# The gate product of an encoder layer as one Strassen level over pairs of token tiles, with the residual tiles kept in memory

## The chip, the core and the metric

One core of a Trainium2 chip runs one layer as one program. The metric is the device time of an execution in microseconds (us); lower is better. The engines work side by side, each through its own list of instructions in order: TensorE (PE in the rows) multiplies matrices into PSUM, VectorE (DVE), ScalarE (ACT) and GpSimd (POOL) do elementwise work, and SyncE (SP) issues the transfers between memory and SBUF. Semaphores order work between engines. All lists are laid down when the program is built, in the order in which the Python code calls the operations.

## The reference: what is computed

```python
xn = rms_norm(x, norm_g[i])
proj = jnp.einsum('bsd,de->bse', xn, w_in[i])
...
oa = diff_attention(q1, q2, k1, k2, va_h, lam, t5_bias)
...
yb = neighbourhood_attention(qb, kb, vb, na_rpb[i]) * jax.nn.silu(zb)
y = jnp.einsum('bse,ed->bsd', jnp.concatenate([ya, yb], axis=-1), w_out[i])
x = x + y
gate = jax.nn.sigmoid(jnp.einsum('bsd,de->bse', x, w_ple_gate[i]))
x = x + gate * jnp.einsum('bsp,pd->bsd', p[i], w_ple_proj[i])
```

There is one batch of 1024 tokens, the model has 1024 columns, and all data are float32. The change concerns the last two lines: the gate product is 1024x1024 by 1024x1024. The residual after the output projection (`x + y`) is called x1 below.

## The kernel before

Every float32 matmul is made of three: an operand is split into a rounded high part and a low part (high by an ACT copy into the type float32r, low by a DVE subtraction), and high x high, high x low and low x high are added up in PSUM. The 1024 tokens are eight tiles of 128. The input projection, neighbourhood attention and differential attention come first. The rest of the program, from about 680 us on, is this:

- `outb` has left the second half of the output projection plus x in a memory tensor `xpd[t]` for each token tile t, with a store `xpd<-oev` for each half tile.
- `outa(t)` loads `xpd[t]` as a tile named x, runs 24 matmuls (`oap`, 128x512 each) for the first half of the output projection, and adds both on DVE (L1231). The result is x1 of that tile, and it stays in SBUF.
- `load_wg` and `split_wg` bring the gate's weights in eight tiles `wgr` of 128x1024 and split them into `wgh` and `wgl`.
- `x1_trans(t)` transposes x1 in eight matmuls with the identity (`x1p`) and splits it into `x1h` and `x1l`.
- `gate(t)` runs, for each half of the columns (c), 24 matmuls into a PSUM tile `gps`, then a tanh on ACT (L1261), then two DVE operations (L1262 with the tile `ppl`, which is half of the embedding's projection and is loaded from memory, and L1263 with x1), and a store to the output.

The order is written out by hand: a loop over t calls `x1_trans(t - 5)`, `gate(t - 6)` and `outa(t)`. SBUF tiles come from pools with a fixed number of buffers for each size; a load into a buffer waits until the last reader of its former content is through. All loads and stores of this stretch are issued by SP, in the order of the code, and SP holds at an instruction whose semaphores have not come.

Of the kernel before, what the change touches and what calls it, by code (L numbers as in the profile page):

```python
# [40 lines left out]
def layer_kernel(ctx, tc, x, p, ngr, w_in, w_out, gains, lamv, t5p, rpbp, w_gate, w_ple,  # L41
# [1155 lines left out]
    wgh = []  # L1197
    wgl = []
    wgr = {}

    def load_wg(kc):
        wgr[kc] = T4([P, D], n="wgr")
        ld(wgr[kc], w_gate[kc * P:(kc + 1) * P, :])

    def split_wg(kc):
        if kc % 2 == 0:
            wgh.append(T8([P, 2, D], F32R, n="wgh"))
            wgl.append(T8([P, 2, D], F32R, n="wgl"))
        r = wgr.pop(kc)
        h, l = wgh[kc // 2], wgl[kc // 2]  # L1210
        act(h[:, kc % 2], r, AF.Copy)
        zl.append(lambda: V.tensor_tensor(l[:, kc % 2], r, h.bitcast(F32)[:, kc % 2], op=OP.subtract))
# [4 lines left out]
    def outa(t):  # L1217
# [14 lines left out]
        x1[t] = xt  # L1232

    def x1_trans(t):
        xt = x1[t]
        h = T4([P, 8, P], F32R, n="x1h")
        l = T4([P, 8, P], F32R, n="x1l")
        for g in range(2):
            tp = PS([P, 4, P], "x1p")
            for k in range(4):  # L1240
                kc = 4 * g + k
                nc.tensor.transpose(tp[:, k], xt[:, kc * P:(kc + 1) * P], idn)
            act(h[:, 4 * g:4 * g + 4], tp, AF.Copy)
            V.tensor_tensor(l[:, 4 * g:4 * g + 4], tp, h.bitcast(F32)[:, 4 * g:4 * g + 4], op=OP.subtract)
        x1T[t] = (h, l)

    def gate(t):
        h, l = x1T.pop(t)
        xt = x1.pop(t)
        for c in range(2):  # L1250
            cs = slice(c * 512, c * 512 + 512)
            pp = T2([P, 512], n="ppl")
            ld(pp, ppd[t][:, cs])
            ps = PS([P, 512], "gps")
            for k in range(8):
                wh, wl = wgh[k // 2][:, k % 2, cs], wgl[k // 2][:, k % 2, cs]
                mm(ps, h[:, k], wh, start=(k == 0), stop=False)  # L1257
                mm(ps, h[:, k], wl, start=False, stop=False)  # L1258
                mm(ps, l[:, k], wh, start=False, stop=(k == 7))  # L1259
            th = T2([P, 512], n="gth")  # L1260
# [76 lines left out]
    for i in range(1, NI + 6):  # L1337
# [39 lines left out]
        if i >= 34:  # L1377
            for kc in (2 * (i - 34), 2 * (i - 34) + 1):
                load_wg(kc)
                if i > 34:  # L1380
                    split_wg(kc - 2)
# [75 lines left out]
```

## Time and profile before

| what | us |
|---|---|
| median of 3 runs | 836.67 |
| the runs, lowest to highest | 835.38 to 838.21 |
| time of the profiled execution | 838.91 |
| its span, first to last instruction | 837.1 |
| TensorE busy in the span | 783.7 (94%) |
| DVE, ACT, POOL busy | 511.8, 437.6, 266.2 |

The profiled execution took 1.81 us more than its span, and 2.24 us more than the median of the runs. Times in the rows below are microseconds from the start of the span. A matmul's shown duration includes its way through the pipeline; how fast matmuls follow each other is read from their starts.

### The profile page before, as it was taken

Reading aid. Unit: us, or ns where it says so; the run is one execution under the profiler, and the core shown is the slowest. Engines: PE = TensorE matmul, PEld = TensorE weight load, DVE = VectorE, ACT = ScalarE, POOL = GpSimd, SP = SyncE. Lnnn points to the kernel's source line nnn. Section 1 sums busy time; section 2 is a strip of 40 time slices with the busy share of each in tenths; the row PEclk is TensorE's granted clock in tenths of the full one; section 3 lists DMA queues with packets and bytes.
Section 4 is the critical chain, followed back from the end, with each engine's and each line's share of the span. In section 5 each row is a group of like instructions: output and inputs, shape, how many; then the busy total and the mean of one; then the engine's idle time right before and its main releaser. Section 6 shows DMA issues by size and latency. Waiting matters only on the chain.

```text
span 837.1 us, 12190 instructions
## 1 busy us (share of the span) xinstructions
PE 783.7 (94%) x4242; PEld 649.8 (78%) x4242; DVE 511.8 (61%) x986; ACT 437.6 (52%) x814; POOL 266.2 (32%) x267
## 2 busy tenths in 40 slices
PE   7899799999989994998979998999999999999997
PEld 6678588888878883776767776888888877888886
DVE  4557795685997662653635658777777752732332
ACT  5665355255435532554545569889888861411120
POOL 1003443261565400110101124677776761200000
PEclk9999899999999997999999999999999999999999
DMA  8655461945788999576666768757686437223222
GB/s 330 272 175 172 170 186 59 325 128 132 173 280 241 217 298 235 140 178 180 200 168 183 175 206 225 216 154 209 163 236 174 144 124 268 85 76 101 83 94 88
DMA packets 118525, 151.94 MB, mean 181 GB/s; under 512 B 23832, under 2 KB 76728, under 8 KB 118336
## 3 DMA queue, kind: packets, MB, share of 16 engines
q1 hardware_dynamic: 116672, 145.39, 59.0%
q0 software_dynamic: 1792, 5.77, 2.2%
q8 instruction: 34, 0.56, 0.3%
q14 instruction: 27, 0.22, 0.1%
HBM read 104.96 MB, written 46.17 MB: 181 GB/s over the span
## 4 chain that ended last, share of the span: by engine, by line
PE 71%; DVE 8%; DMA 7%; ACT 5%; issue 4%; SPq 2%; POOL 2%; ACTq 0%; DVEq 0%; POOLq 0%
PE ips L232 7%; PE ips L234 7%; PE ips L233 7%; PE dsp L1064 6%; PE gps L1259 3%; PE gps L1257 3%; PE gps L1258 3%; PE dtp L1106 3%; DMA uad<-zth 3%; PE ntp L683 3%; PE pps L312 2%; PE zps L580 2%; PE zps L582 2%; PE zps L581 2%; DMA Vw<-vb 2%
## 5 line engine op out<-in xcount | busy, mean ns | idle before, releaser
L232 PE MATMUL ips<-w,xh 128*128 128x512 f32 x336 | 135.0, 402 | 5.6 <-DVE C L258 4.1
L234 PE MATMUL ips<-w,xl 128*128 128x512 f32 x336 | 132.5, 394 | 0.0
L233 PE MATMUL ips<-w,xh 128*128 128x512 f32 x336 | 132.3, 394 | 0.0
L1089 POOL TENSOR_TENSOR s<-s,s 128x1024 f32<-128x1024 f32 x32 | 77.0, 2408 | 56.9 <-ACT s L1088 52.3
L431 POOL TENSOR_TENSOR qrs<-qms,nhalf 128x16 f32<-128x16 f32 x16 | 51.7, 3233 | 91.5 <-DVE qms L429 91.5
L1074 DVE CUSTOM_DVE_ANT_0 s<-dsp,T 128x1024 f32<-128x1024 f32 x64 | 77.7, 1215 | 2.5 <-PE dsp L1064 2.5
L232 PEld LDWEIGHTS ips<-w,xh 128*128 128x128 f32 x336 | 64.2, 191 | 19.3 <-issue 4.8
L1076 ACT ACTIVATE s<-s,dm 128x1024 f32<-128x1024 f32 x64 | 73.4, 1146 | 4.6 <-DVE dm L1074 4.5
L234 PEld LDWEIGHTS ips<-w,xl 128*128 128x128 f32 x336 | 63.9, 190 | 13.9
L233 PEld LDWEIGHTS ips<-w,xh 128*128 128x128 f32 x336 | 64.2, 191 | 13.1 <-DVE w L216 0.3
L1064 PE MATMUL dsp<-K,Q 128*128 128x512 f32 x256 | 69.7, 394 | 4.9 <-DVE dm L1074 4.3
L1113 DVE TENSOR_TENSOR aTl<-dtp,aTh 128x512 fp32r<-128x512 f32 x64 | 44.2, 691 | 46.9 <-ACT aTh L1107 46.9
L714 POOL TENSOR_TENSOR yb<-nay,yb 128x128 fp32r<-128x128 f32 x32 | 16.2, 508 | 174.5 <-ACT yb L713 174.5
L216 DVE TENSOR_TENSOR w<-wraw,w 128x512 fp32r<-128x512 f32 x84 | 62.2, 778 | 5.9 <-ACT w L215 5.4
L1064 PEld LDWEIGHTS dsp<-K,Q 128*128 128x128 f32 x256 | 45.9, 189 | 14.6 <-issue 3.0
L685 ACT ACTIVATE PT<-ntp 96x768 f32<-96x768 f32 (+1 forms) x32 | 25.9, 810 | 59.2 <-PE ntp L683 59.2
L580 PE MATMUL zps<-xh,zw 128*128 128x512 f32 x128 | 54.3, 424 | 0.0
L582 PE MATMUL zps<-xh,zw 128*128 128x512 f32 x128 | 51.1, 399 | 0.0
L581 PE MATMUL zps<-xl,zw 128*128 128x512 f32 x128 | 51.0, 398 | 0.0
L215 ACT ACTIVATE w<-wraw 128x512 fp32r<-128x512 f32 x84 | 48.4, 625 | 4.7 <-DVE wraw L191 4.5
L1257 PE MATMUL gps<-wgh,x1h 128*128 128x512 f32 x128 | 50.5, 395 | 0.0
L1107 ACT ACTIVATE aTh<-dtp 128x512 fp32r<-128x512 f32 x64 | 38.0, 593 | 23.1 <-PE dtp L1106 23.1
(174 smaller groups left out, 1823.2 us busy)
## 6 DMA issues: line engine op xcount, KB each, us to landing
wraw<-in_w_in_dram SPq DMA_DIRECT2D x72, 256.0 KB
x<-in_x_dram SPq DMA_DIRECT2D x8, 512.0 KB
ppd<-pp SPq DMA_DIRECT2D x8, 512.0 KB
K<-kbh SPq DMA_DIRECT2D x8, 512.0 KB
Q<-qbh SPq DMA_DIRECT2D x16, 256.0 KB
Q<-qah SPq DMA_DIRECT2D x16, 256.0 KB
Q<-qal SPq DMA_DIRECT2D x16, 256.0 KB
wor<-in_w_out_dram SPq DMA_DIRECT2D x8, 512.0 KB
```

The lines of the kernel that those rows point to most:

```text
L216: V.tensor_tensor(w[:, 1], r, w.bitcast(F32)[:, 0], op=OP.subtract)
L232: mm(ps, lh[:, k, a:a + P], w[:, 0], start=(new and k == 0), stop=False, skip_group_check=cont)
L233: mm(ps, lh[:, k, a:a + P], w[:, 1], start=False, stop=False, skip_group_check=cont)
L234: mm(ps, ll[:, k, a:a + P], w[:, 0], start=False, stop=(k == 3), skip_group_check=cont)
L580: mm(ps, w[:, 0, kc], xh(kc, a, b), start=(kc == 0), stop=False)
L581: mm(ps, w[:, 0, kc], xl(kc, a, b), start=False, stop=False)
L582: mm(ps, w[:, 1, kc], xh(kc, a, b), start=False, stop=(kc == 7))
L1064: mm(ps[:, cs], q[g][:, m, u * P:(u + 1) * P], k[:, cs], start=(g == 0), stop=(g == 1))
L1074: V.tensor_tensor_reduce(out=s, in0=ps, in1=back(Td[h][:, :], 1919 - (896 - P * qt), [[-1, S]]), scale=-1.0, scalar=BIG, op0=OP.add, op1=O ...
L1076: act(s, s, AF.Exp, bias=mx, scale=-1.0, accum_out=z[:, m:m + 1])
L1089: G.tensor_tensor(s1, s1, s2, op=OP.add)
L1257: mm(ps, h[:, k], wh, start=(k == 0), stop=False)
```

## The change

x1 is seen as a 2x2 matrix of blocks: tile p of the first four token tiles and tile q = p + 4 of the last four give the rows, the two halves of the 1024 inputs give the columns. The gate's weights are a 2x2 matrix of quarters (B11 to B22, 512x512). The product of the two is made with one level of Strassen's scheme in Winograd's form: seven block products (P1 to P7) for eight, each 12 matmuls of 128x512, so 7 x 12 x 4 pairs = 336 matmuls take the place of 384. In return:

- Four sums of weight quarters (T1 to T4) and four sums of x1 blocks (S1 to S4) are formed, and each of the seven operands on either side is split into high and low: `g_first` (B11, B21, T1, T2), `g_second` (T3, B22, and T4 as a sum), `g_left1` to `g_left3` for the x1 side. Sums run on POOL and DVE, splits on ACT and DVE. The weights come as 16 loads of 128x512 for the first set and the same 16 again for the second set.
- Two PSUM halves A and B of one tile `gab` and one tile C (`gps`) hold the products; P6 and P7 go on top of A, P3 on top of B, P4 on top of A. Between them ACT copies A or B out (`gwv`, `gxy`), and DVE adds copies to PSUM.
- `outa(t)` stores x1 back to `xpd[t]` as soon as it is added. Tiles 0 and 4 are also used from SBUF; the other six are loaded again by `x1_load` before their transposes. The last addition of each half tile reads x1 from memory once more (`x1r`, loaded by `g_pre` beside `ppl`).

In the built program every product on `gab` waits for the last engine that read that tile, whichever half was read: P5 (which starts B) waits for the ACT copy of A behind P6, P7 (on A) for the copy of B behind P5, P3 (on B) for the copy of A behind P7, and P4 (on A) for the DVE addition behind P3.

```diff
--- before.py
+++ after.py
@@ -1194,22 +1194,48 @@
         G.tensor_tensor(yl[:, h % 2, cs], y, yh.bitcast(F32)[:, h % 2, cs], op=OP.subtract)
 
 
...
+
+
+    GLEFT = dict(P1="A11", P2="A12", P6="S2", P5="S1", P7="S3", P3="S4", P4="A22")
+    GRIGHT = dict(P1="B11", P2="B21", P6="T2", P5="T1", P7="T3", P3="B22", P4="T4")
+    gw = {}
+    gr = {}
+    gl = {}
+
+    def g_load(k, names):
+        for n in names:
+            i, j = int(n[1]) - 1, int(n[2]) - 1
+            gr[n, k] = T2([P, 512], n="wgr")
+            ld(gr[n, k], w_gate[(4 * i + k) * P:(4 * i + k + 1) * P, j * 512:(j + 1) * 512])
+
+    def g_tiles(*names):
+        for n in names:
+            gw[n] = (T8([P, 4, 512], F32R, n="wgh"), T8([P, 4, 512], F32R, n="wgl"))
+
+    def g_split(n, k, r):
+        h, l = gw[n]
+        act(h[:, k], r, AF.Copy)
+        V.tensor_tensor(l[:, k], r, h.bitcast(F32)[:, k], op=OP.subtract)
+
+    def g_first(k):
+        a, b, c, d = [gr.pop((n, k)) for n in ("B11", "B12", "B21", "B22")]
+        G.tensor_tensor(b, b, a, op=OP.subtract)
+        g_split("B11", k, a)
+        g_split("B21", k, c)
+        G.tensor_tensor(d, d, b, op=OP.subtract)
+        g_split("T1", k, b)
+        g_split("T2", k, d)
+
+    def g_second(k):
+        a, b, c, d = [gr.pop((n, k)) for n in ("B11", "B12", "B21", "B22")]
+        V.tensor_tensor(b, d, b, op=OP.subtract)
+        g_split("T3", k, b)
+        G.tensor_tensor(a, a, b, op=OP.add)
+        G.tensor_tensor(c, c, a, op=OP.subtract)
+        g_split("B22", k, d)
+        gr["T4", k] = c
+
+    QUARTERS = ("B11", "B12", "B21", "B22")
 
     x1 = {}
     x1T = {}
@@ -1229,39 +1255,126 @@
                 mm(ps, yh[:, k % 2, a:b], wl, start=False, stop=False)
                 mm(ps, yl[:, k % 2, a:b], wh, start=False, stop=(k == 3))
         V.tensor_tensor(xt, pss, xt, op=OP.add)
...
+        st(xpd[t], xt)
+        if t % 4 == 0:
+            x1[t] = xt
+
+    def x1_load(t):
+        x1[t] = TA([P, D], n="x1")
+        ld(x1[t], xpd[t])
+
+    lt = {}
+
+    def l_split(p, n, src):
+        w = T4([P, 2, 4, P], F32R, n="x1s")
+        gl[p, n] = w
+        act(w[:, 0], src, AF.Copy)
+        V.tensor_tensor(w[:, 1], src, w.bitcast(F32)[:, 0], op=OP.subtract)
+
+    def g_left1(p):
+        pa = [PS([P, 4, P], "x1p") for _ in range(2)]
+        pb = PS2([P, 2, 4, P], "x1q")
+        pts = pa + [pb[:, 0], pb[:, 1]]
+        for i in range(4):
+            xt = x1[p + 4 * (i // 2)]
             for k in range(4):
...
+                kc = 4 * (i % 2) + k
+                nc.tensor.transpose(pts[i][:, k], xt[:, kc * P:(kc + 1) * P], idn)
+        x1.pop(p)
+        x1.pop(p + 4)
+        f = TA([P, 2, 4, P], n="x1f")
+        e = TA([P, 2, 4, P], n="x1e")
+        lt[p] = (f, e)
+        act(f[:, 0], pts[0], AF.Copy)
+        act(f[:, 1], pts[1], AF.Copy)
+        act(e[:, 0], pts[2], AF.Copy)
+        V.tensor_tensor(e[:, 1], pts[3], e[:, 0], op=OP.add)
+        l_split(p, "A22", pts[3])
+        l_split(p, "A11", f[:, 0])
+        l_split(p, "A12", f[:, 1])
+        V.tensor_tensor(e[:, 0], f[:, 0], e[:, 0], op=OP.subtract)
+        l_split(p, "S1", e[:, 1])
+        V.tensor_tensor(e[:, 1], e[:, 1], f[:, 0], op=OP.subtract)
+
+    def g_left2(p):
+        f, e = lt[p]
+        l_split(p, "S2", e[:, 1])
+        l_split(p, "S3", e[:, 0])
+        V.tensor_tensor(e[:, 1], f[:, 1], e[:, 1], op=OP.subtract)
+
+    def g_left3(p):
+        l_split(p, "S4", lt.pop(p)[1][:, 1])
+
+    def g_prod(p, ps, n, new):
+        w = gl.pop((p, GLEFT[n]))
+        h, l = gw[GRIGHT[n]]
+        c = not new
+        for k in range(4):
+            mm(ps, w[:, 0, k], h[:, k], start=(new and k == 0), stop=False, skip_group_check=c)
+            mm(ps, w[:, 0, k], l[:, k], start=False, stop=False, skip_group_check=c)
+            mm(ps, w[:, 1, k], h[:, k], start=False, stop=(k == 3), skip_group_check=c)
+
+    def g_pre(t, c):
+        cs = slice(c * 512, c * 512 + 512)
+        pp, xr = T2([P, 512], n="ppl"), T2([P, 512], n="x1r")
+        ld(pp, ppd[t][:, cs])
+        ld(xr, xpd[t][:, cs])
+        return pp, xr
+
+    def g_fin(t, c, src, pre, th=None):
+        cs = slice(c * 512, c * 512 + 512)
+        pp, xr = pre
+        th = T2([P, 512], n="gth") if th is None else th
+        act(th, src, AF.Tanh, scale=0.5)
+        V.scalar_tensor_tensor(th, th, 1.0, pp, op0=OP.add, op1=OP.mult)
+        V.tensor_tensor(xr, th, xr, op=OP.add)
+        ld(out[t * P:(t + 1) * P, cs], xr)
+
+    def gate(p, extra):
+        q = p + 4
+        nxt = p + 1 < 4
+        if nxt:
+            x1_load(p + 1)
+            x1_load(q + 1)
+        ab = PS2([P, 2, 512], "gab")
+        A, B = ab[:, 0], ab[:, 1]
+        C = PS([P, 512], "gps")
+        wv = TA([P, 2, 512], n="gwv")
+        xy = TA([P, 2, 512], n="gxy")
+        g_prod(p, A, "P1", True)
+        act(wv[:, 0], A, AF.Copy)
+        extra(0)
+        pre = g_pre(p, 0)
+        g_prod(p, C, "P2", True)
+        th = T2([P, 512], n="gth")
+        V.tensor_tensor(th, C, wv[:, 0], op=OP.add)
+        g_fin(p, 0, th, pre, th)
+        extra(1)
+        g_prod(p, A, "P6", False)
+        act(xy[:, 0], A, AF.Copy)
+        if nxt:
+            g_left1(p + 1)
+        g_prod(p, B, "P5", True)
+        act(wv[:, 1], B, AF.Copy)
+        extra(2)
+        pre = g_pre(q, 1)
+        g_prod(p, A, "P7", False)
+        act(xy[:, 1], A, AF.Copy)
+        th = T2([P, 512], n="gth")
+        V.tensor_tensor(th, xy[:, 1], wv[:, 1], op=OP.add)
+        g_fin(q, 1, th, pre, th)
+        if nxt:
+            g_left2(p + 1)
+        pre = g_pre(p, 1)
+        g_prod(p, B, "P3", False)
+        th = T2([P, 512], n="gth")
+        V.tensor_tensor(th, B, xy[:, 0], op=OP.add)
+        g_fin(p, 1, th, pre, th)
+        if nxt:
+            g_left3(p + 1)
+        pre = g_pre(q, 0)
+        g_prod(p, A, "P4", False)
+        g_fin(q, 0, A, pre)
 
     NI = 32
 
@@ -1374,23 +1487,40 @@
         if not even:
             if 0 <= (i - 5) // 2 < NP:
                 d_ss((i - 5) // 2)
...
+        if i == 34:
+            g_load(0, QUARTERS)
+        if i >= 35:
+            if i == 35:
+                g_tiles("B11", "B21", "T1", "T2")
+            g_load(i - 34, QUARTERS)
+            g_first(i - 35)
+    z_low()
+    outa(5)
+    g_first(3)
+    g_left1(0)
+    g_load(0, QUARTERS)
+    outa(6)
+    g_left2(0)
+    g_left3(0)
+    outa(7)
+    g_tiles("T3", "B22", "T4")
+
+    def extra(j):
+        if j == 0:
+            g_load(2, QUARTERS)
+            g_second(1)
+        elif j == 1:
+            g_load(3, QUARTERS)
+            g_second(2)
+            g_second(3)
+        else:
+            for k in range(4):
+                g_split("T4", k, gr.pop(("T4", k)))
+
+    g_load(1, QUARTERS)
+    g_second(0)
+    for p in range(4):
+        gate(p, extra if p == 0 else lambda j: None)
 
 
 def _consts():
```

The change moves instructions on several engines; three places are shown. The first is SP's list while the output projection's tiles 1 to 3 are worked on (`x` is the tile that `outa` loads from `xpd`, `wgr` a piece of the gate's weights). Before:

```order
L97 DMA x_1567_7144<-xpd_2846 128x1024
L97 DMA wgr_7197<-in_w_gate_dram 128x1024
L97 DMA wgr_7199<-in_w_gate_dram 128x1024
L97 DMA x_1574_7205<-xpd_2847 128x1024
L97 DMA wgr_7243<-in_w_gate_dram 128x1024
L97 DMA wgr_7248<-in_w_gate_dram 128x1024
L97 DMA x_1586_7263<-xpd_2848 128x1024
```

The same place now:

```order
L97 DMA x_1567_7145<-xpd_2846 128x1024
L100 DMA xpd_2846<-x_1567_7145 128x1024
L97 DMA wgr_7199<-in_w_gate_dram 128x512
L97 DMA wgr_7201<-in_w_gate_dram 128x512
L97 DMA wgr_7203<-in_w_gate_dram 128x512
L97 DMA wgr_7205<-in_w_gate_dram 128x512
L97 DMA x_1576_7211<-xpd_2847 128x1024
L100 DMA xpd_2847<-x_1576_7211 128x1024
```

The store of tile 1's x1 stands ahead of four loads of weights and of the load of x for tile 2, and so on for each tile up to 7; before, no store stood among these loads.

The second place is ACT's list around the first gate. Before, it holds the splits of transposed x1 and the tanh of each half tile:

```order
L1243 ACTIVATE x1h_7396<-x1p_7398 128x512
L1243 ACTIVATE x1h_7396<-x1p_7405 128x512
L1261 ACTIVATE gth_7439<-gps_7414 128x512
L1261 ACTIVATE gth_7471<-gps_7446 128x512
L1243 ACTIVATE x1h_7504<-x1p_7506 128x512
```

Now, from the copy of A behind P1 (L1345) to the copy of A behind P6 (L1354) and the first copy of the next pair's transposes; L1217 are splits of T3 and B22 for the blocks 1, 2 and 3 of their rows, L1328 is the tanh:

```order
L1345 ACTIVATE gwv_7568<-gab_7566 128x512
L1217 ACTIVATE wgh_7541<-wgr_7549 128x512
L1217 ACTIVATE wgh_7543<-wgr_7553 128x512
L1328 ACTIVATE gth_7614<-gth_7614 128x512
L1217 ACTIVATE wgh_7541<-wgr_7585 128x512
L1217 ACTIVATE wgh_7543<-wgr_7589 128x512
L1217 ACTIVATE wgh_7541<-wgr_7622 128x512
L1217 ACTIVATE wgh_7543<-wgr_7626 128x512
L1354 ACTIVATE gxy_7569<-gab_7566 128x512
L1288 ACTIVATE x1f_7674<-x1p_7655 128x512
```

Six splits of second-set weights and one tanh now stand between the copy behind P1 and the copy behind P6.

The third place is SP's list from one gate to the next, with the stores to the output and the loads for the half tiles' ends. Before:

```order
L97 DMA ppl_7708<-ppd_95 128x512
L97 DMA out_dram<-x_1586_7263 128x512
L97 DMA ppl_7740<-ppd_95 128x512
L97 DMA out_dram<-x_1586_7263 128x512
L97 DMA ppl_7788<-ppd_96 128x512
L97 DMA out_dram<-x_1592_7301 128x512
```

Now, from the first pair's second store (q, second half) to the second pair's first store:

```order
L97 DMA out_dram<-x1r_7716 128x512
L97 DMA ppl_7745<-ppd_92 128x512
L97 DMA x1r_7746<-xpd_2845 128x512
L97 DMA out_dram<-x1r_7746 128x512
L97 DMA ppl_7770<-ppd_96 128x512
L97 DMA x1r_7771<-xpd_2849 128x512
L97 DMA out_dram<-x1r_7771 128x512
L97 DMA x_1680_7791<-xpd_2847 128x1024
L97 DMA x_1681_7793<-xpd_2851 128x1024
L97 DMA ppl_7812<-ppd_93 128x512
L97 DMA x1r_7813<-xpd_2846 128x512
L97 DMA out_dram<-x1r_7813 128x512
```

Each store is now followed by two loads for the next half tile, and the two loads of x1 for the next pair's transposes stand behind the pair's last store.

## Rows read from the trace of the kernel before

**Rows 1.** Windows view: busy time by engine, clock, DMA share and rate.

```profile
core 0: us, PE busy (x) PEld busy (x) DVE busy (x) ACT busy (x) POOL busy (x), PEclk, DMA share, GB/s
700.00:712.00 12.00, 12.00 (x69) 10.41 (x68) 3.27 (x5) 1.38 (x3) 0.51 (x1) 1.00 1.03 411
728.16:832.00 103.84, 103.71 (x483) 85.97 (x481) 34.39 (x49) 16.16 (x30) 0.00 (x0) 1.00 0.26 87
```

**Rows 2.** Timeline of TensorE: start, us, line, operation, count.

```profile
721.04 1.04 PE L1242 MATMUL x1p<-idn,x 128*128 128x128 f32 x8
721.83 0.48 PE L1228 MATMUL oap<-woh,yah 128*128 128x512 f32 x1
...
797.24 1.03 PE L1242 MATMUL x1p<-idn,x 128*128 128x128 f32 x8
798.03 0.47 PE L1257 MATMUL gps<-wgh,x1h 128*128 128x512 f32 x1
...
809.04 1.03 PE L1242 MATMUL x1p<-idn,x 128*128 128x128 f32 x8
```

**Rows 3.** Timeline of ScalarE in the gates; brackets: idle time before, releaser.

```profile
809.23 0.60 ACT L1261 ACTIVATE gth<-gps 128x512 f32<-128x512 f32 x1 [4.79 <-PE gps L1259]
809.73 1.09 ACT L1243 ACTIVATE x1h<-x1p 128x512 fp32r<-128x512 f32 x2
...
831.91 0.60 ACT L1261 ACTIVATE gth<-gps 128x512 f32<-128x512 f32 x1 [4.84 <-PE gps L1259]
```

**Rows 4.** Timeline of VectorE: an x1 addition, split subtractions, the last gate's end.

```profile
709.41 1.23 DVE L1231 TENSOR_TENSOR x<-oap,x 128x1024 f32<-128x1024 f32 x1 [4.99 <-PE oap L1230]
...
811.20 1.28 DVE L1244 TENSOR_TENSOR x1l<-x1p,x1h 128x512 fp32r<-128x512 f32 x2
...
832.54 0.69 DVE L1262 SCALAR_TENSOR_TENSOR gth<-gth,ppl 128x512 f32<-128x512 f32 x1 [4.02 <-ACT gth L1261]
833.27 0.69 DVE L1263 TENSOR_TENSOR x<-gth,x 128x512 f32<-128x512 f32 x1
```

**Rows 5.** Timeline of SP's issues: start, us to issue.

```profile
696.42 0.39 SPq L97 DMA_DIRECT2D x<-xpd  x1
696.90 0.87 SPq L97 DMA_DIRECT2D wgr<-in_w_gate_dram  x2
...
782.27 0.34 SPq L97 DMA_DIRECT2D out_dram<-x  x1
782.65 0.42 SPq L97 DMA_DIRECT2D ppl<-ppd  x1
...
833.99 0.34 SPq L97 DMA_DIRECT2D out_dram<-x  x1
```

**Rows 6.** Chain that ended last, in order of time: start, us, what.

```profile
687.18 0.33 SPq L100
...
687.56 3.66 DMA x<-xpd
...
694.62 0.23 PE oap L1228
...
697.01 0.43 PE oap L1229
```

**Rows 7.** Windows view around one output store and one `ppl` load (columns as in Rows 1).

```profile
783.00:785.75 2.75, 2.75 (x15) 2.27 (x14) 0.00 (x0) 0.12 (x1) 0.00 (x0) 1.00 0.55 190
785.75:788.00 2.25, 2.25 (x15) 1.95 (x14) 1.70 (x3) 1.47 (x3) 0.00 (x0) 1.00 0.00 1
```

**Rows 8.** Line groups of GpSimd: a sum of two 128x512 tiles.

```profile
L1037 POOL TENSOR_TENSOR oev<-oev,xr 128x512 f32<-128x512 f32 x16 | 20.9, 1304 | 0.7 <-ACT oev L1036 0.7
```

**Rows 9.** Windows of TensorE alone: us, PE busy, clock, DMA share, GB/s.

```profile
692.00:694.00 2.00, 0.81 (x6) 1.00 0.00 0
696.00:698.00 2.00, 2.00 (x6) 0.50 0.58 180
```

**Rows 10.** Timeline of TensorE just before the low clock.

```profile
693.19 0.61 PE L1154 MATMUL dss<-ones,osq 128*128 128x1 f32 x4 [1.59 <-DVE aTl L1113]
```

More of the change, by code (lines that the diff above doesn't have):

```diff
@@ L1194, in d_y @@
         G.tensor_tensor(yl[:, h % 2, cs], y, yh.bitcast(F32)[:, h % 2, cs], op=OP.subtract)
[L1197 to L1212, printed above, removed]
+    GLEFT = dict(P1="A11", P2="A12", P6="S2", P5="S1", P7="S3", P3="S4", P4="A22")
[32 more added lines that the diff above has]
+    QUARTERS = ("B11", "B12", "B21", "B22")
     x1 = {}
@@ L1231, in outa @@
         V.tensor_tensor(xt, pss, xt, op=OP.add)
[L1232 to L1239, printed above, removed]
-            for k in range(4):
[L1241 to L1260, printed above, removed]
-            act(th, ps, AF.Tanh, scale=0.5)
-            V.scalar_tensor_tensor(th, th, 1.0, pp, op0=OP.add, op1=OP.mult)
-            V.tensor_tensor(xt[:, cs], th, xt[:, cs], op=OP.add)
-            ld(out[t * P:(t + 1) * P, cs], xt[:, cs])
+        st(xpd[t], xt)
@@ L1376, in layer_kernel @@
                 d_ss((i - 5) // 2)
[L1377 to L1381, printed above, removed]
-    for t in range(5, 8 + 6):
-        z_low()
-        if t == 5:
-            split_wg(6)
-            z_low()
-            split_wg(7)
-        if 0 <= t - 5 < 8:
-            x1_trans(t - 5)
-        if t >= 6:
-            gate(t - 6)
-        if t < 8:
-            outa(t)
+        if i == 34:
[30 more added lines that the diff above has]
+        gate(p, extra if p == 0 else lambda j: None)
 def _consts():
```

## The prediction

> **What bounds the kernel now.** I read the windows view of the stretch with the gates first: TensorE is busy for 103.71 of 103.84 us at a clock of 1.00, DVE for a third of it, ACT for a sixth, POOL not at all, and the DMA engines are a quarter busy [rows 1]. So the gates end when TensorE has issued its last matmul. Then the timelines, to see what one thing costs. From one tile's transposes to the next are 11.80 us, of which eight transposes take 0.79; the 48 matmuls between take 11.01, so 0.229 each [rows 2]. ACT needs 0.60 for one 128x512 read of PSUM and 0.55 in a row of two [rows 3]. DVE needs 0.69, 0.73 from start to start where one feeds the next, 0.6 where not, and 1.23 for an x1 addition [rows 4].
>
> Last I looked at SP, since the change touches its list most. SP sends what it has as fast as it can (two pieces of weights 0.5 us after a load of x), and holds only where a store waits for its data: the output store leaves at 782.27, and the next `ppl` load 0.38 later [rows 5]. No load stands behind a store that matters: each `ppl` is needed some 5 us later.
>
> **What the change removes.** 48 matmuls of 0.229: 11.0 us, all on TensorE, which is the bound. Transposes are as many as before. Without any new wait the span would be 826.1.
>
> **What it adds.** Elementwise work (about 76 more DVE operations of 0.6, some 50 ACT ones, 16 POOL sums of 1.30 [rows 8]) fits by amount: DVE would have about 80 us in the 150 from the late output projection on. I cost the amount at nothing; engines that stood idle cover it. What costs is order: in four places a list holds at something late, and everything behind it is late too. A product is 12 x 0.229 = 2.75, a pair's 16 transposes 1.6, so a pair without waits is 20.85 (19.25 the last, which transposes nothing), against 23.6 for two tiles now.
>
> For transfers I take two prices. A 512 KB load right behind a 256 KB store landed 691.22 - 687.18 = 4.04 after the store's issue (687.56 + 3.66) [rows 6]. The new `ppl` and `x1r` after a store have the same sizes together. The lower bound is 3.48: the traffic of one `ppl` behind one store is over at 785.75 [rows 5, 7]. I take 3.8 for the first of the two. Then come 0.73 and 0.69 on DVE, so one store follows the last after 5.2 (4.9 to 5.5). In bulk the engines move 411 GB/s [rows 1]; to bytes over 411 I add 1.3 for start and landing (0 below; 4.04 less 0.79 MB over 411 is 2.1 above).
>
> **1. Output projection.** x for tile t + 1 now stands behind the store of tile t's x1 and four pieces of weights: 2.10 MB, 5.1 us, with 1.3 and the addition's 1.23 that is 7.6 from one addition's end to the next (6.3 to 8.4), where TensorE needs 24 x 0.229 = 5.5. Tile 2's addition still waits for TensorE and ends at 710.64 [rows 4]; with 7.6 a tile, tile 5's ends at 733.4. TensorE starts tile 5 at 721.0 (the transposes at 721.04 [rows 2] are gone from there), is through at 726.5, transposes the first pair until 728.1, and finds the PSUM buffer for tile 6 taken until tile 5's addition: 5.3 us of waiting (1.4 to 7.7). Two tiles of 5.5 later, at 744.4, P1 starts.
>
> **2. First pair, P5.** P5 waits for the ACT copy of A behind P6, and ACT has splits of T3 and B22 of blocks 1 to 3 ahead of it. Block 3's weights are issued behind the pair's first output store. Tile 6's addition ends 7.6 after tile 5's, at 741.0; tile 7's x stands behind one store (1.05 MB, 2.55 + 1.3) and is added by 746.1. From there SP has a store of x1, eight pieces of weights, two x1 tiles, `ppl` and `x1r` to move, 4.19 MB: 10.2 + 1.3, so 757.6. Two DVE operations, 759.0, the store; then block 3's weights, 1.31 MB with the store, 3.2 + 1.3: 763.5. A DVE sum, two splits and the copy (0.69 + 0.60 + 0.55 + 0.60): 765.95. TensorE would have been ready at 744.4 + 3 x 2.75 + 1.6 = 754.25. Waiting: 11.7 (8 to 14, by the same bounds taken three times).
>
> **3. P7, P3, P4 of each pair.** P7 waits for the copy of B, which stands on ACT behind three copies and four splits of the next pair, with a DVE sum between: 1.65 + 0.69 + 2.2 + 0.6 = 5.15 after P6's copy, while P5 takes 2.75: 2.4 of waiting. P3 waits for a copy after P7's end: 0.16 + 0.60, so 0.75. P4 waits for the DVE addition behind P3, ahead of which DVE has the end of half tile (q, second half), two subtractions and a sum: from the copy 0.73 + 0.62 + 0.73 + 0.73 + 1.8 + 0.69 = 5.3, less P3's 2.75: 2.55. First pair in all: 11.7 + 2.4 + 0.75 + 2.55 = 17.4.
>
> **4. Pairs two and three.** Counted from the end of the copy behind P7 (c): the first store leaves at c + 2.8, P4 ends at c + 8.05. Each next store is a round trip of 5.2 later, since its loads stand behind the one before: c + 8.0 and c + 13.2. Behind that stand the x1 tiles, 1.31 MB with the store: c + 17.7. TensorE has done P1, P2, P6 at c + 16.3 and reaches the second tile's transposes at c + 17.1: 0.6 of waiting. `ppl` and `x1r` for the new pair land 1.3 later, at c + 19.0, and DVE holds there, ahead of the sum that the A22 split needs; c + 20.4 for the two operations, then 0.69 + 2.2 + 0.6: the copy ends at c + 23.9 where P5 is done at c + 21.25, 2.65 of waiting instead of 2.4. With P3 and P4: 6.55 a pair, 13.1 for two. A pair is then 27.4, more than two tiles now.
>
> **5. Last pair and end.** No transposes hide or push anything: three copies, 0.75 each, and for P4 0.85 (c + 3.6 against 2.75): 3.1. P4 ends at 744.4 + 3 x 20.85 + 19.25 + 17.4 + 13.1 + 3.1 = 859.8. Now 833.99 to the end of the span is 3.1 [rows 5]; without late loads the end would be 859.8 + 0.16 + 0.60 + 0.05 + 0.73 + 0.69 + 3.1 = 865.1. But the last three stores are round trips: c is 853.45, the stores leave at 856.25, 861.45 and 866.65, and the end is 869.75: 4.65 more.
>
> **Sum.** 837.1 - 11.0 + 5.3 + 17.4 + 13.1 + 3.1 + 4.65 = 869.65, a span 32.5 longer. The profiled execution took 838.91, so the like one would take 871.5; the median of the runs was 836.67, 2.24 below it, and I predict against that: 869.
>
> **A price left out of the sum: the clock.** After TensorE had waited 1.59 us at 693.19 [rows 10], the granted clock fell from 1.00 to 0.50 [rows 9], that is from 2.4 to 1.2 GHz, and about eight matmuls followed each other at 0.43 instead of 0.23 [rows 6]: 1.6 us. The new waits are longer than that one. But P5 at half speed runs while the copy behind it is late anyway, and the two long waits of steps 1 and 2 end on transfers, not on TensorE, so I count 0 and keep 1.6 for each wait as the upper bound. The Trainium skill ("TensorE: Matmul & The Clock Gate", HAM oscillation) describes a kernel in which each short group of matmuls was followed by a wait for data and began again at the slow clock, group after group. By that rule the change would pay after each wait, and the sum would be that of the third rival, 882 for 869. The trace agrees in the one case at 693.19 and cannot show the repetition.
>
> **Rivals.**
> - Faster: the waits are covered, TensorE stays the bound. For it: TensorE at 103.71 of 103.84 with DMA a quarter busy [rows 1]. Against it: the order shows SP's stores ahead of the loads. It decides at 11.0 us of waiting in all; with none, 837.1 - 11.0, a time near 826. Chance 0.05.
> - Start only: transfers are late in steps 1 and 2, but from the second pair on loads land in time, so only the copies and P4's addition show (0.75 + 0.75 + 0.85, twice, 4.7 for 13.1), the wait before tile 6 is at its lower end (1.4) and the end loses 2 fewer: 869 - 8.4 - 3.9 - 2 = 855. For it: a lone load's traffic is over 3.1 us after its issue [rows 5, 7]. Against: three round trips in a row a pair. Chance 0.10.
> - Clock: half speed after P7's and P4's waits in each pair, 8 x 1.6 = 12.8: 882. For it: rows 9. Against: those products are often followed by another wait that hides it. Chance 0.13.
> - My forecast, 869 (857 to 876 by the bounds of steps 1 to 5): 0.72.
>
> **Range and chances.** 850 to 884 leaves out the faster case and the outer ends of the start and clock cases, about 15 in 100. A measurement of this kernel tells 0.3% (2.5 us) from no change. Faster 0.05; same 0.01, a sum of waits that falls on 11.0; slower 0.94.
>
> **What would show it.** TensorE idle for some 5 us before tile 6's `oap`, over 8 us before the first pair's P5, released by ACT's L1354; pairs 27 us apart; in each pair idle time before P7 and P4 of over 2 us; x loads and weights issued right after stores; stores at the end 5 us apart. Wrong would be pairs under 23.6 apart, or a first pair under 30 us. If the clock is below 1.00 through the pairs, the third rival is right.

## The result, and the profile after

The changed kernel takes 892.28 us in the median (four runs, 886.30 to 892.73) beside 836.23 for the kernel before: a ratio of 1.065, 95% interval 1.060 to 1.070. 869 was predicted, in a range of 850 to 884. The direction was right and the size was not. The profiled execution took 892.73, its span is 891.0.

The windows view of after (columns as in [rows 1]):

```profile
723.30:730.40 7.10, 6.13 (x32) 4.92 (x30) 2.85 (x4) 0.64 (x1) 0.49 (x1) 1.00 0.86 294
...
760.00:770.00 10.00, 4.83 (x23) 3.44 (x23) 5.32 (x5) 2.70 (x5) 5.07 (x4) 0.95 0.97 324
...
700.00:720.00 20.00, 20.00 (x104) 17.06 (x103) 8.01 (x9) 4.08 (x8) 4.66 (x6) 1.00 0.67 224
720.00:740.00 20.00, 10.20 (x48) 7.77 (x46) 10.85 (x11) 5.50 (x11) 9.16 (x10) 0.79 0.63 215
...
760.00:780.00 20.00, 6.53 (x29) 4.74 (x28) 11.96 (x11) 4.48 (x8) 8.51 (x6) 0.73 0.83 280
...
820.00:840.00 20.00, 17.00 (x70) 13.18 (x68) 8.54 (x13) 6.17 (x11) 0.00 (x0) 0.91 0.50 165
```

Where TensorE was busy for 103.71 of 103.84 us before [rows 1], it is now busy for 10.20 of 20 in the output projection and for 6.53 of 20 in the first pair. Its timeline shows before which products it waits, and who ends the wait (in brackets):

```profile
732.43 1.97 PE L1282 MATMUL x1q<-idn,x 128*128 128x128 f32 x8 [3.00 <-DVE x L1257]
742.14 0.80 PE L1254 MATMUL oap<-woh,yah 128*128 128x512 f32 x1 [7.74 <-DVE x L1257]
...
754.58 0.39 PE L1313 MATMUL gab<-wgh,x1s 128*128 128x512 f32 x1
...
768.40 1.39 PE L1282 MATMUL x1p<-idn,x 128*128 128x128 f32 x8 [3.73 <-DMA x<-xpd]
...
782.71 0.80 PE L1313 MATMUL gab<-wgh,x1s 128*128 128x512 f32 x1 [11.02 <-ACT gxy L1354]
783.30 0.63 PE L1314 MATMUL gab<-wgl,x1s 128*128 128x512 f32 x1
783.73 0.63 PE L1315 MATMUL gab<-wgh,x1s 128*128 128x512 f32 x1
...
797.30 0.50 PE L1313 MATMUL gab<-wgh,x1s 128*128 128x512 f32 x1 [2.60 <-DVE gth L1371]
...
826.23 0.50 PE L1313 MATMUL gab<-wgh,x1s 128*128 128x512 f32 x1 [2.23 <-DVE gth L1371]
...
827.40 0.63 PE L1314 MATMUL gab<-wgl,x1s 128*128 128x512 f32 x1
827.83 0.63 PE L1315 MATMUL gab<-wgh,x1s 128*128 128x512 f32 x1
...
854.62 0.79 PE L1313 MATMUL gab<-wgh,x1s 128*128 128x512 f32 x1 [2.24 <-DVE gth L1371]
855.21 0.63 PE L1314 MATMUL gab<-wgl,x1s 128*128 128x512 f32 x1
855.64 0.63 PE L1315 MATMUL gab<-wgh,x1s 128*128 128x512 f32 x1
```

Three of these waits are the ones that the prediction named: tile 6, P5 behind the copy L1354, P4 behind the addition. The 3.00 and 3.73 before transposes were not named. Against its own working (P4's times follow from its sums):

| start of | predicted | measured | late by |
|---|---|---|---|
| first P1 | 744.4 | 754.58 | 10.2 |
| first P5 | 765.95 | 782.71 | 16.8 |
| P4 of pairs 1 to 4 | 779.9, 807.3, 834.7, 857.05 | 797.30, 826.23, 854.62, 879.20 | 17.4, 18.9, 19.9, 22.2 |
| end of span | 869.65 | 891.0 | 21.35 |

So 16.8 of the 21.35 us arise before the first P5, in steps 1 and 2. SP's and VectorE's timelines show one hop from tile to tile there, and the store on which P5 hangs. The additions (L1257) are those of tiles 2, 4, 5 and 7:

```profile
722.79 0.33 SPq L100 DMA_DIRECT2D xpd<-x  x1
723.16 2.28 SPq L97 DMA_DIRECT2D wgr<-in_w_gate_dram  x4
725.49 0.42 SPq L97 DMA_DIRECT2D x<-xpd  x1
732.40 0.33 SPq L100 DMA_DIRECT2D xpd<-x  x1
...
774.50 0.34 SPq L97 DMA_DIRECT2D out_dram<-x1r  x1
774.94 1.81 SPq L97 DMA_DIRECT2D wgr<-in_w_gate_dram  x4
```

```profile
711.45 1.23 DVE L1257 TENSOR_TENSOR x<-oap,x 128x1024 f32<-128x1024 f32 x1 [6.87 <-DMA x<-xpd]
...
731.15 1.23 DVE L1257 TENSOR_TENSOR x<-oap,x 128x1024 f32<-128x1024 f32 x1 [5.00 <-DMA x<-xpd]
...
740.86 1.23 DVE L1257 TENSOR_TENSOR x<-oap,x 128x1024 f32<-128x1024 f32 x1 [2.17 <-DMA x<-xpd]
...
758.01 1.22 DVE L1257 TENSOR_TENSOR x<-oap,x 128x1024 f32<-128x1024 f32 x1 [3.10 <-DMA x<-xpd]
...
780.30 0.69 DVE L1231 TENSOR_TENSOR wgr<-wgr,wgr 128x512 f32<-128x512 f32 x1 [1.61 <-DMA wgr<-in_w_gate_dram]
```

From store to store are 9.61 us, where 7.6 were predicted: 0.5 until bytes move, 7.1 at 294 GB/s, 0.75 to landing, 1.23 for the addition. The order of events is the one predicted, and so are the 1.3 us for start and landing; the price of the bytes is not.

A part of the lateness is older than the change. Tile 0's addition, up to which SP's transfers are the same in both kernels, starts at 693.15 here and at 691.32 in the trace of the kernel before; in the traces of the experiments it lies between 689.7 and 695.4.

### The profile page after: what moved, and what is told of

Its sections match the earlier page's. It is cut to its first block, busy times and chain, and to the rows that moved or that the text cites. A ratio compares the mean times of both kernels' runs of the same rounds, so it can differ in the third digit from the quotient of the medians.

```text
span 891.0 us, 12370 instructions
## 1 busy us (share of the span) xinstructions
PE 788.0 (88%) x4194; PEld 647.1 (73%) x4194; DVE 559.4 (63%) x1050; ACT 468.9 (53%) x874; POOL 288.3 (32%) x283
## 4 chain that ended last, share of the span: by engine, by line
PE 57%; DMA 15%; DVE 10%; issue 5%; ACT 5%; SPq 3%; POOL 3%; DVEq 0%; POOLq 0%; ACTq 0%
PE ips L232 6%; PE ips L234 6%; PE ips L233 6%; PE dsp L1064 6%; DMA ppl<-ppd 3%; SPq L97 3%; DMA uad<-zth 3%; PE dtp L1106 3%; PE ntp L683 2%; PE zps L580 2%; PE zps L582 2%; PE zps L581 2%; DMA x<-xpd 2%; PE npv L698 2%; PE dpv L1133 2%
## 5 line engine op out<-in xcount | busy, mean ns | idle before, releaser
L1313 PE MATMUL gab<-wgh,x1s 128*128 128x512 f32 x96 | 41.5, 432 | 28.4 <-ACT gxy L1354 11.7
```

## Experiments

My theory: SP's order makes loads stand behind stores, at places that can be removed one by one, and the bulk transfers were priced too cheaply. Rivals: the bytes themselves are the bound, or the new work on VectorE and ScalarE, or the shared PSUM tile. The diffs are abridged, and their comments were added for this text.

| run | median us | ratio to the kernel before (95%) |
|---|---|---|
| e1_defer | 881.55 | 1.051 (1.047 to 1.055) |
| e2_rows | 885.24 | 1.055 (1.050 to 1.060) |
| e3_pre | 885.71 | 1.056 (1.052 to 1.060) |
| e4_psum | 884.07 | 1.054 (1.050 to 1.058) |
| e5_pre_psum | 872.24 | 1.041 (1.038 to 1.044) |
| e6_defer_rows | 877.89 | 1.048 (1.045 to 1.052) |
| e7_noset2 | 871.74 | 1.041 (1.038 to 1.044) |
| e8_all | 858.95 | 1.025 (1.022 to 1.028) |
| e9_early | 846.10 | 1.009 (1.007 to 1.011) |
| e10_order | 843.55 | 1.007 (1.005 to 1.009) |
| e11_act | 841.03 | 1.003 (1.001 to 1.005) |
| e12_noset2 | 828.96 | 0.989 (0.987 to 0.991) |
| e13_vec | 840.08 | 1.002 (1.001 to 1.004) |
| e14_copy | 841.55 | 1.005 (1.003 to 1.006) |

Gains below are differences from 892.28 where nothing else is said. The kernel before, run beside each, had medians of 836.2 to 838.6, so differences of about 2 us between runs of different groups tell nothing.

**e1: x1's stores one tile later.**

```diff
 def outa(t):
     ld(xt, xpd[t])
+    flush()                      # st() of the tile before
...
-    st(xpd[t], xt)
+    held.append((xpd[t], xt))
```

> The only edit: the store of a token tile's x1 is queued on SP one tile later, behind the next tile's x load instead of ahead of it. Theory 1 (order): SP holds each store until VectorE's addition, so the four weight pieces and the next x start too late, and the 9.3 to 10.1 us from x1 store to x1 store is a round trip. Then TensorE's waits of 3.00 and 7.74 us in the output projection go, the first gate product starts 10 us earlier than at 754.6, and the time is 880 to 884 us. Theory 2 (bandwidth): one tile's 2 MB take the hop whatever their order; the stores still come 8 us or more apart, and the time is 888 to 893 us. In both, the four pairs take what they took.

10.7 us less. The waits of 3.00 and 7.74 became one of 4.59, and P1 starts at 747.4:

```profile
733.56 0.80 PE L1261 MATMUL oap<-woh,yah 128*128 128x512 f32 x1 [4.59 <-DVE x L1264]
```

So the larger part of step 1's wait was SP's order: the same bytes, moved past one store, come that much earlier.

**e2: the first weight set in rows of 4 KB.**

```diff
-    ld(gr[n, k], w_gate[rows, j * 512:(j + 1) * 512])
+    ld(w, w_gate[rows, :])      # 128x1024, halves used as before
```

> The only edit: the first of the two weight sets is fetched in pieces of 128 x 1024 (rows of 4 KB, two transfers for a block row) instead of 128 x 512 (rows of 2 KB, four transfers), the same bytes in the same place of SP's list. Theory 1 (row size): the pieces of 2 KB ran at about 300 GB/s where 411 were counted; with 4 KB the traffic of a hop falls from 7.0 to some 5.1 us, four or five hops get 2 us shorter each, and the time is 882 to 886 us. Theory 2 (the mixture of stores and loads sets the rate, or SP's hold does): hops stay at 9.3 to 10.1 us and the time at 890 to 893 us.

7.0 us less, a time within theory 1, but not by its way: a hop fell from 9.6 to 9.2 (stores at 718.95 and 728.16), not by 2. The output projection ends 4.2 earlier and P5 starts 6.5 earlier, but 2.5 of either stands already at tile 0's addition (690.68 for 693.15), ahead of the edit. So the row size is a part of the price only.

**m_rows: the price by itself.**

```diff
+stage(lambda: narrow(0, buf[0]), lambda: narrow(1, buf[1]))
+stage(lambda: broad(0, buf[0]), lambda: broad(1, buf[1]))
+stage(lambda: xstore(buf[3]), lambda: narrow(0, buf[0]), lambda: xload(buf[2]))
```

> The changed kernel, and behind its end six stages of transfers alone, each started when the one before has landed: 2 MB of weights in 128 x 512 pieces; the same in 128 x 1024 pieces; the tile hop's loads (1 MB of weights in 128 x 512 pieces, then 512 KB of x) without the 512 KB store ahead of them, and with it; and both again with 128 x 1024 pieces. Theory 1 (row size): rows of 2 KB move at 310 to 330 GB/s and rows of 4 KB at 400 to 415, with or without the store. Theory 2 (mixture): both row sizes move at about 400 alone, and fall to about 300 only with the store ahead. If both count, narrow loads alone are near 325 and the store takes the rate of either below 350.

The windows view of the stages, each cut to its traffic: narrow alone, broad alone, the hop's narrow loads without and with the store, the broad ones without and with it.

```profile
907.60:914.40 6.80, 0.00 (x0) 0.00 (x0) 1.23 (x1) 0.00 (x0) 0.00 (x0) 0.50 0.88 305
920.30:926.40 6.10, 0.00 (x0) 0.00 (x0) 1.23 (x1) 0.00 (x0) 0.00 (x0) 0.50 0.88 332
932.80:937.60 4.80, 0.00 (x0) 0.00 (x0) 0.38 (x1) 0.00 (x0) 0.00 (x0) 0.50 0.89 315
943.00:949.60 6.60, 0.00 (x0) 0.00 (x0) 0.42 (x1) 0.00 (x0) 0.00 (x0) 0.50 0.89 313
955.20:959.90 4.70, 0.00 (x0) 0.00 (x0) 0.93 (x1) 0.00 (x0) 0.00 (x0) 0.50 0.93 330
964.80:970.60 5.80, 0.00 (x0) 0.00 (x0) 0.00 (x0) 0.00 (x0) 0.00 (x0) 0.50 0.96 350
```

Neither theory's sizes hold. In this one run, bursts of 1.6 to 2.1 MB move at 305 to 350 GB/s; 2 KB rows cost about a tenth, and the store ahead slows nothing. None reaches the 411 of [rows 1], which I had read from 12 us full of transfers.

**e3 and e4: the pairs.**

```diff
-        g_fin(q, 1, th, pre, th)          # e3: loads of the next half tile ahead
+        nx = g_pre(p, 1)
+        g_fin(q, 1, th, pre, th)
...
-        A, B = ab[:, 0], ab[:, 1]         # e4: B in a tile of its own
+        A, B = ab[:, 0], PS([P, 512], "gpb")
```

> The only edit: the two loads that a gate half tile needs (ple product and x1) are queued on SP ahead of the output store of the half tile before, not behind it. Theory 1 (round trips on SP): the stretch from one output store to the next was a store's wait, a load and VectorE's three operations (4.7 to 5.9 us); without it P4's wait falls from 2.2 to 2.6 us to some 0.8, the waits before the next pair's transposes go, the pairs take 25 us for 28.4 to 28.9, and the time is 881 to 886 us. Theory 2 (the shared TensorE buffer of A and B sets the pair): P7, P3 and P4 wait as before for copies and additions, and the time is 888 to 893 us.

> The only edit: the two product sums A and B stand in two tiles of their own instead of two halves of one, so that a product into one does not wait for a copy or an addition that reads the other. Theory 1 (shared tile): P7, P3 and P4 lose their waits (0.7 to 1.6, 0.7 and 2.2 to 2.6 us in each pair), P5 of the first pair no longer waits for the copy behind the weight splits and the wait of 11 us moves to P7 and gets 2.7 us shorter; the time is 875 to 881 us. Theory 2 (round trips on SP): the lost waits come back before the next pair's first products, since VectorE makes their operands behind additions that wait for loads; the time is 886 to 892 us.

e3 gave 6.6 and left P4's wait at 2.24 (theory 1 had 0.8), though the later pairs' waits for x went. e4 gave 8.2: the waits before P7, P3 and P4 went, and this came in their place, in TensorE's timeline of e4:

```profile
809.01 1.97 PE L1282 MATMUL x1p<-idn,x 128*128 128x128 f32 x8 [7.87 <-DMA x<-xpd]
```

Each hides a part of the other. So the two together:

> The two edits on the pairs together: loads of the next half tile ahead of the output store, and A and B in tiles of their own. Alone they gave 6.6 and 8.2 us of the 892.3. Theory 1 (two holds in series: with A and B apart, the waits came back as 7.9 and 3.9 us for the next pair's x, which stands behind output stores): together they give more than their sum, the later pairs take 22 to 23.5 us each, and the time is 870 to 875 us. Theory 2 (independent): their sum, 877 to 879 us.

20.0 for the 14.8 of both alone. Two holds in series: whoever takes one away sees only a part of its worth.

**e6: e1 and e2 together**, the two edits above.

> The two edits on the output projection together: x1's stores one tile later in SP's list, and the first weight set in rows of 4 KB. Alone they gave 10.8 and 7.1 us. With the stores later, one wait of 4.59 us for an x load is left before tile 6, behind weight pieces that themselves wait for buffers. Theory 1 (transfer rate): the wider pieces take 3 to 4 us of it, and the time is 877 to 879 us. Theory 2 (what is left is no matter of the rate): 880 to 883 us. If the two were independent it would be 874.5.

14.4 less, at the value of theory 1; but the wait before tile 6 stayed at 4.87. What the traces have earlier than in e1 stands in front of every edit (tile 0's addition at 689.66 for 693.57); from there to the end of the span e6 takes 185.7 us and e1 184.3. That the wider rows give anything on top of e1 is not shown.

**e7: no second weight set.**

```diff
-    g_load(1, QUARTERS)
-    g_second(0)
+    gw["T3"], gw["B22"], gw["T4"] = gw["T2"], gw["B21"], gw["B11"]
```

> Leaves out the whole second weight set (the second reading of 4 MB, its differences and its splits): T3, B22 and T4 are replaced by tiles of the first set, so the product is not the reference's. All else as after the change. Theory 1: P5's wait of 11.0 us, P6's of 1.4 and most of the 3.7 for x before pair one's transposes belong to the second set; the time is 874 to 878 us, and pairs two to four take what they took. Theory 2 (behind that wait stands another one as long, the round trip from the first output store or the operands of pair one): 884 to 890 us.

20.5 less, more than expected: P5 and P6 wait for nothing, and the later pairs keep their waits (1.63, 0.69 and 2.24 in pair two). So step 2's wait belongs to the second set, its loads, sums and splits taken together.

**e8: all together**, and P5 ahead of the splits of blocks two and three.

```diff
-        extra(1)
         g_prod(p, A, "P6", False)
...
         act(wv[:, 1], B, AF.Copy)
+        extra(1)
         extra(2)
```

> All the edits together (x1 stores later, wide rows for the first weight set, loads of the next half tile ahead of the store, A and B apart), and in the first pair the copy of A and the whole of P5 ahead of the splits of weight blocks two and three. Theory 1 (each hold is a place of its own): out-projection 11 to 15 us less, pairs 18 to 20 less, first pair 3 to 5 less: 853 to 861 us. Theory 2 (behind all of them stands one common bound, the bytes that go through the DMA engines in this stretch): 866 to 872 us.

33.3 less. No common bound stands behind the holds down to here. What is left: 4.6 us at tile 6, 5.45 and 3.87 within P7, 5.4 for x in two pairs.

**e9: loads as early as their buffers allow.**

```diff
+        if t < 7:
+            xld(t + 1)
...
+    for k in (2, 3):
+        w = T8([P, 4, 512], n="wgz")     # block rows of the second set, 4 KB rows
```

> On top of all the edits together (858.95 us): each x load of the output projection one tile earlier, the splits of first-set weight block two behind tile 5's addition; the x loads of the next pair queued right behind the transposes of the pair before, not behind an output store; and the second weight set's blocks zero and one read during the output projection, blocks two and three in rows of 4 KB into two buffers that come free at its end. Theory 1 (the waits still seen are SP's order): of 4.6 us at tile 6, 9.3 and 1 at P7, and 2.8 and 2.6 at the transposes some 15 go, and the time is 840 to 847 us. Theory 2 (for the second set the 16 differences and 12 splits on VectorE, GpSimd and ScalarE take that long, whenever the data come): P7 still waits 6 us or more, and the time is 848 to 854 us.

12.9 less again, within theory 1. No wait of TensorE ends on a transfer any more; 3.93 at tile 7 and 8 within P7 end on VectorE and ScalarE.

**e10 and e11: the order on VectorE, GpSimd and ScalarE.**

```diff
     outa(5)
+    g_left1(0)
     g_first(2)
...
-        V.tensor_tensor(b, d, b, op=OP.subtract)     # e10: differences of set two
+        G.tensor_tensor(b, d, b, op=OP.subtract)
...
-    g_sp("T30", "T31", "B220", "B221")               # e11: behind the copy of P1
+        if j == 0:
+            g_sp("T30", "T31", "B220", "B221")
```

> On top of the version before (846.1 us), whose left waits of 3.9 us at tile 7 and 8 us at P7 ended on VectorE and ScalarE, no longer on a transfer: the first pair's transposes and operands are made ahead of the splits of first-set blocks two and three; GpSimd takes all differences of the second set, those of blocks zero and one during the output projection; and the splits come in the order in which the products want them (T3, B22, T4). Theory 1 (what is left is the order of VectorE's work): both waits and the half clock behind them go to 3 us in all or less, and the time is 832 to 838 us, below the 838.3 of the kernel before or equal to it. Theory 2 (VectorE's amount of work between 727 and 770 us is the bound): the waits move to P1, P3 or the second pair's first product, and the time is 841 to 845 us.

> On top of the version before (843.6 us), whose two waits left (6.0 us at P6 and 3.8 at P3 of the first pair) ended on ScalarE's copies of P1 and P5 behind weight and operand splits: the copy of P1 goes ahead of the second set's first splits, and in the first pair the making of pair two's operands goes behind P5's copy. Theory 1 (ScalarE's order): both waits go, and the time is 834 to 839 us. Theory 2 (VectorE's amount of work from 740 to 780 us, 35 of 40 us busy, with its operations drawn out while GpSimd works): the waits come back at P7, P3 or pair two's first product, and the time is 841 to 845 us.

Both fell to theory 2. In e10 the two waits named went, and 6.05 at P6 and 3.76 at P3 stand in their place; in e11 these shrink to 3.97 and 0.56, and 1.01 at P7 and 2.88 at P4 come up. The timelines of VectorE and GpSimd in e11 show why VectorE is late:

```profile
739.08 5.79 DVE L1227 TENSOR_TENSOR wgl<-wgw,wgh 128x512 fp32r<-128x512 f32 x4
750.60 6.59 DVE L1227 TENSOR_TENSOR wgl<-wgr,wgh 128x512 fp32r<-128x512 f32 x4
```

```profile
739.15 1.77 POOL L1245 TENSOR_TENSOR wgr<-wgr,wgr 128x512 f32<-128x512 f32 x1
741.00 1.62 POOL L1246 TENSOR_TENSOR wgr<-wgr,wgr 128x512 f32<-128x512 f32 x1
742.58 1.74 POOL L1245 TENSOR_TENSOR wgr<-wgr,wgr 128x512 f32<-128x512 f32 x1
```

Four subtractions take 5.8 to 6.6 us beside GpSimd's, where 0.6 each was counted [rows 4]. That GpSimd is the reason is tested in e13.

**e12: e10 without the second weight set**, replaced as in e7.

> The version of 843.6 us without the second weight set: no second reading, differences or splits, T3, B22 and T4 replaced by tiles of the first set (so the product is not the reference's). Theory 1 (the second set is all that now stands between the 48 matmuls saved and the end): the two waits of 9.8 us and the half clock behind them go, and the time is 828 to 833 us, 5 to 10 us below the kernel before. Theory 2 (the pairs themselves, with operands, copies and x by way of memory, cost as much as the matmuls saved): 836 us or more.

828.96, and TensorE's row of the windows view is as full as before the change:

```profile
740.00:760.00 20.00, 20.00 (x99) 16.75 (x98) 14.55 (x23) 8.97 (x16) 0.00 (x0) 1.00 0.66 218
760.00:780.00 20.00, 20.00 (x98) 16.79 (x97) 13.48 (x21) 9.97 (x18) 0.00 (x0) 1.00 0.60 197
```

So the 48 matmuls are worth 9.6 us of the 11.0 counted (10.0 by the spans of the two traces, whose tile 0 additions stand at 691.36 and 691.32). The second set is all that keeps e10 from it; whether by its loads or by its sums and splits, this run can't tell.

**e13 and e14: VectorE without GpSimd beside it, and one copy earlier.**

```diff
-        G.tensor_tensor(c, c, a, op=OP.subtract)     # e13
+        V.tensor_tensor(c, c, a, op=OP.subtract)
...
-        if not p:                                     # e14: behind the copy of P7
-            left(p)
         g_prod(p, A, "P7", False)
         act(xy[:, 1], A, AF.Copy)
+        if not p:
+            left(p)
```

> On top of the version of 841.0 us: the twelve differences of the second weight set (T3 and T4) move from GpSimd to VectorE, those of T4 behind the splits of T3 and B22. In the run before, VectorE's 128 x 512 subtractions took 1.71 us each while GpSimd worked and 0.69 alone, GpSimd's 1.6 to 1.75. Theory 1 (the two engines hinder each other, so that GpSimd's share costs VectorE more than it takes off it): each subtraction falls to 0.69 to 0.72 us, VectorE has 12 more operations (8.3 us) and gets some 8 to 9 us back, and the time is 837 to 841 us. Theory 2 (VectorE's subtractions are slow there for another reason, such as their input or the traffic beside them): they stay above 1 us, VectorE falls 8 us further behind, and the time is 845 to 850 us.

> On top of the version of 840.1 us, whose one wait left (8.6 us before P4 of the first pair) ended on ScalarE's copy behind P7, which stood behind four splits of T4 and the seven copies and splits of pair two's operands: that copy goes ahead of pair two's operands. Theory 1 (ScalarE's order): P4 can start once T4 is split, about 4.3 us earlier, pair two's first product then waits 1 to 2 us for its operands, and the time is 835 to 838 us, at or a little below the kernel before. Theory 2 (VectorE's amount of work in the first pair): what P4 gains pair two's first product loses, and the time is 839 to 842 us.

e13's VectorE timeline answers the open question: four subtractions at 739.70 take 2.48, and so on through the pair.

```profile
739.70 2.48 DVE L1227 TENSOR_TENSOR wgl<-wgw,wgh 128x512 fp32r<-128x512 f32 x4
747.70 2.49 DVE L1227 TENSOR_TENSOR wgl<-wgr,wgh 128x512 fp32r<-128x512 f32 x4
```

But VectorE now does GpSimd's twelve as well, and the time stays (840.08 for 841.03). e13's one wait, before P4, and the longest wait of e14, before P6 of pair two:

```profile
767.71 0.80 PE L1343 MATMUL gab<-wgh,x1s 128*128 128x512 f32 x1 [8.59 <-ACT gxy L1401]
```

```profile
775.22 0.80 PE L1343 MATMUL gab<-wgh,x1s 128*128 128x512 f32 x1 [4.54 <-ACT gwv L1380]
```

In e14 the 8.59 became 1.85 at P7, 2.30 at P4, and 0.60 and 4.54 at P1 and P6 of pair two: the sum is 9.3, as theory 2 had it. VectorE, third in this row of e14's windows view, is hardly ever idle while the second set is made:

```profile
740.00:760.00 20.00, 17.11 (x83) 13.70 (x81) 17.91 (x29) 8.97 (x16) 0.00 (x0) 1.00 0.76 272
```

With the second set made in the first pair, the amount of VectorE's work is then the likeliest thing to hold the end. That is argued from these rows and from e12: most of the waits themselves end on ScalarE's copies, and no run made the second set in less of VectorE's time. No version that computes the reference beat the kernel before.

## Why the prediction was right, and where it was wrong

- The saving of 48 matmuls: nearly right. With every wait gone (e12) 9.6 us of the 11.0 are there; the span is 827.1 where 826.1 was worked out.
- Step 1, the hold before tile 6: right in place and, for the larger part, in cause (e1), wrong in size. **The step that failed is the price of bulk transfers**, "in bulk the engines move 411 GB/s". The hop moved its 2.10 MB at 294 GB/s, in 7.1 us for 5.1, so it took 9.61 from store to store for 7.6, outside the bounds of 6.3 to 8.4; m_rows has 305 to 350 GB/s for such bursts alone. Tile 2's addition waited for its x, not for TensorE as worked out, and ended 2.0 late (1.8 of this was there at tile 0); the next three hops took 29.4 for 22.8, so tile 5's addition ended at 742.09, 8.7 late. Tiles 6 and 7 then took 12.4 for 11.0, beginning at half clock: the first P1 came 10.2 late.
- Step 2, P5 behind the copy behind block three's weights: right in cause (e7), and late by the same term. Tile 7's addition ended 13.1 late (759.23 for 746.1; its own load took 7.5 for 5.1), from there to the output store were 15.3 us for 12.9, from there to P5 8.2 for 6.95. These add up to the 16.8.
- Step 3: right for the first pair's P3 and P4, 0.69 and 2.60 beside 0.75 and 2.55. P7's wait was 0.69 for 2.4 since P5 ran its first matmuls 0.43 apart and so took up 1.7 of it; in pairs two and three it was 1.62, under the 2 us named as a sign. e4 confirms what was read from the built program: these waits are there because A and B are one PSUM tile.
- Step 4: 28.9 and 28.4 for 27.4 a pair. The stores' round trips were right (4.7 to 5.9, in the mean 5.1, for 5.2). Pair two's transposes waited 2.2 for x where 0.6 was worked out, again a bulk load: 6.1 from the store to the second tile's transposes for 4.5.
- Step 5: 24.6 from P4 to P4 where its terms give 22.35, of which 1.6 is the clock at the first of the two, and the tail 0.8 shorter.
- The clock was to be 0 and could have been 12.8. Six waits had the lower level behind them (512-column matmuls 0.43 apart, or eight transposes in up to 1.97 us instead of 1.03): those of 3.00 and 3.73 before transposes, of 7.74 before tile 6, of 11.02 before P5, and of 2.23 and 2.24 before P4 of pairs two and three. At tile 6, P5 and the two P4 that cost about 1.6 us each; P5's was covered by P7's wait, as foreseen, the two P4's were not. After 2.60 before P4 of pair one, and after the 1.62 before P7 in pairs two and three, the clock stayed up. The rule of the Trainium skill ("TensorE: Matmul & The Clock Gate", HAM oscillation) holds in part: of the eight places of the third rival, P7 and P4 of each pair, two came. The third rival as a whole did not come.
- "I cost the amount at nothing; engines that stood idle cover it" did not show in the changed kernel, whose holds were longer. In the stretch in which the second set is made it does not hold: e10 to e14, with SP's holds gone, end on VectorE's and ScalarE's work for that set.

What stays open: why the same engines moved 411 to 414 GB/s around 700 to 710 (before, and in e8) and no whole burst of m_rows did.

## What to carry to other kernels

Fewer operations on the engine that sets the end gain nothing as long as one engine's list (here SP's) holds loads behind stores of data that are made late; look for each place where a load stands behind such a store, and move the load, before counting the saving. Holds in series hide each other, so take away pairs of them (6.6 and 8.2 alone, 20.0 together). Price a burst of transfers by a burst of like size, rows and beginning in the trace, not by the best sustained stretch. Count elementwise work against the stretch in which it has to be done, not against the idle time of the whole: the second set's had to fit into the first pair.

## What the runs showed of the hardware

VectorE and GpSimd slow each other. A 128x512 float32 subtraction with both inputs in SBUF took 0.68 us on VectorE alone (e13) and 1.5 to 1.8 beside GpSimd's (e11), and GpSimd's took 1.6 to 1.8 for 1.3 alone (both in e11). The Trainium skill ("SBUF — State Buffer", Who interferes with whom) states that a VectorE instruction with two SBUF inputs contends with a GpSimd instruction that reads SBUF, since its second input comes through the read interface that the two share, and calls the shared port pair an exclusive lock. The trace agrees nearly: strictly in turns, 0.68 and 1.29 would give 1.97 for one of each, and the rows have 1.6 to 1.8. Two such operations one behind the other on VectorE take 1.3: here GpSimd's help was a loss for VectorE, though the kernel's time was the same without it (e13).

After the wait of 11.02 us the first matmuls of P5 came 0.43 apart, from the ninth on 0.23: the price of one such wait was 1.7 us, nearly the 1.6 read from the kernel before. P4 of pairs two and three lost 1.6 each behind waits of 2.23 and 2.24 us, so not only the long waits had this price.
